# Instance norm on one core: the first store leaves as a 2 KB-per-row transfer and a 30 KB-per-row transfer

## The chip, the core and the metric

The kernel runs on one core of a Trainium2 chip. A core has four compute engines that matter here: TensorE (PE in the profile, with its weight loads as PEld), VectorE (DVE), ScalarE (ACT) and GpSimd (POOL), and SyncE (SP), which here only issues transfers. Tensors live in HBM. Work is done in the on-chip buffer SBUF, which has 128 partitions, and in the accumulation memory PSUM. Sixteen DMA engines move data between HBM and SBUF. An engine that issues transfers has a queue of them; the profile calls SP's queue q1 and ACT's queue q10, and each of the two reaches all 16 DMA engines.

The metric is the device time of one execution in microseconds (us), and lower is better.

## The reference

The input x has the shape 4 x 8 x 16 x 256 x 256 in float32: 512 channels of 65,536 numbers, 134 MB. Each channel is normalised by its own mean and variance and multiplied by its own gamma.

```python
mu = x.mean(axis=(3, 4), keepdims=True)
var = ((x - mu) ** 2).mean(axis=(3, 4), keepdims=True)
x_norm = (x - mu) / np.sqrt(var + 1e-5)
out = x_norm * gamma[None, :, :, None, None]
```

Every number is read once and written once: 134 MB in, 134 MB out.

## The kernel before

**Tiles.** The 512 channels are cut into 32 units of 16 channels. A unit is one tile `xt` of 128 partitions x 8192 float32 (4 MB): each channel takes 8 partitions, and each partition holds one row of 32 KB that is contiguous in HBM. There are six such tiles in SBUF (`slots`, `AHEAD = 6`), and unit u lives in slot u % 6.

**Start.** Line 54 issues the loads of units 0 to 5 at once: units 1 and 3 on ACT's queue, units 0, 2, 4 and 5 on SP's. Gamma comes in by a small transfer from GpSimd (line 52) and is spread over the partitions by 16 small matmuls (line 83) into `g_col`.

**The loop over units (lines 100 to 131).** For each unit:
- line 102, VectorE: the sum of each row, into `st[:, u, 0]`
- line 103, ScalarE: the sum of squares of each row, into `st[:, u, 1]`; the squares themselves go to a throw-away tile `junk`
- line 111, TensorE: a matmul with the constant `navg` adds up the 8 rows of each channel and hands every partition minus the mean and minus the mean square, in `ps`
- lines 112, 116, 120 and 122: four small operations on VectorE, ScalarE, VectorE, VectorE that give `scale` = gamma / sqrt(var + eps)
- line 125, VectorE: the tile is normalised in place
- line 129, ScalarE's queue: the store of the tile
- line 131, SP's queue (through line 48): the load of unit u + 6 into the slot that the store of unit u leaves

**What sets the order.** Each engine runs its instructions in the order in which they are written here. Waits between engines are semaphores that the framework puts in. The load of unit u + 6 waits on SP until the store of unit u has landed, as both use one slot. Every large transfer signals its landing on one of eight semaphores, which the framework hands out in turn, in the order of the program: the six first loads, the store of unit 0, the load of unit 6, the store of unit 1, the load of unit 7, and so on. Before a transfer takes a semaphore again, its issuing engine waits until the previous transfer on that semaphore has landed. For a store in the middle of the kernel that previous transfer is the store four units earlier.

In SBUF a whole tile is one row per partition, so the transfer of a tile is 128 pieces of 32 KB, eight for each DMA engine, and one 4-byte piece on each engine for the semaphore.

Of the kernel before, what the change touches and what calls it, by code (L numbers as in the profile page):

```python
# [1 line left out]

# [4 lines left out]

F32 = mybir.dt.float32
U8 = mybir.dt.uint8
ALU = mybir.AluOpType  # L10
ACTF = mybir.ActivationFunctionType
AX = mybir.AxisListType


@with_exitstack
def kernel(
    ctx: ExitStack,
    tc: tile.TileContext,
    x: bass.AP,
    gamma: bass.AP,  # L20
    out: bass.AP,
):
    nc = tc.nc
    B, G, C, H, W = x.shape
    P = nc.NUM_PARTITIONS
    HW = H * W
    n_ch = B * G * C
    S = 8
    K = P // S
    F = HW // S  # L30
    U = n_ch // K
    NG = (G * C) // K
    AHEAD = 6
    assert HW % S == 0 and (G * C) % K == 0

    xv = x.rearrange("b g c h w -> (b g c h w)").rearrange("(u p f) -> u p f", p=P, f=F)
    ov = out.rearrange("b g c h w -> (b g c h w)").rearrange("(u p f) -> u p f", p=P, f=F)
    gv = gamma.rearrange("g c -> (g c)")

    data = ctx.enter_context(tc.tile_pool(name="data", bufs=1))  # L40
    singles = ctx.enter_context(tc.tile_pool(name="singles", bufs=1))
    psum = ctx.enter_context(tc.tile_pool(name="psum", bufs=4, space=bass.MemoryType.PSUM))
    ctx.enter_context(tc.manual_schedule())

    slots = [data.tile([P, F], F32, name=f"xt{i}") for i in range(AHEAD)]

    def load(u, queue):
        queue.dma_start(out=slots[u % AHEAD][:], in_=xv[u])  # L48


    g_row = singles.tile([1, G * C], F32, name="g_row")
    nc.gpsimd.dma_start(out=g_row[:], in_=gv[None, :])  # L52
    for u in range(AHEAD):
        load(u, nc.scalar if u in (1, 3) else nc.sync)


    eps_t = singles.tile([P, 1], F32, name="eps_t")
    nc.gpsimd.memset(eps_t[:], 1e-5)  # L58
    one = singles.tile([1, 1], F32, name="one")
    nc.gpsimd.memset(one[:], 1.0)  # L60
    navg = singles.tile([P, K, S], F32, name="navg")
    nc.gpsimd.memset(navg[:], -1.0 / HW)  # L62
    nc.gpsimd.affine_select(  # L63
        out=navg[:], in_=navg[:], pattern=[[-S, K], [0, S]], compare_op=ALU.is_ge,
        fill=0.0, base=0, channel_multiplier=1,
    )
    nc.gpsimd.affine_select(  # L67
        out=navg[:], in_=navg[:], pattern=[[S, K], [0, S]], compare_op=ALU.is_ge,
        fill=0.0, base=S - 1, channel_multiplier=-1,
    )  # L70
    navg_w = navg[:].rearrange("p k s -> p (k s)")
    root_eps = singles.tile([P, 1], F32, name="root_eps")
    nc.scalar.activation(out=root_eps[:], in_=eps_t[:], func=ACTF.Sqrt)  # L73
    g_rep = singles.tile([1, NG, K, S], F32, name="g_rep")
    g_ps = psum.tile([P, NG], F32, name="g_ps", bufs=1)
    g_col = singles.tile([P, NG], F32, name="g_col")

    nc.vector.tensor_copy(  # L78
        out=g_rep[:],
        in_=g_row[:].rearrange("o (n k) -> o n k", n=NG).unsqueeze(3).to_broadcast([1, NG, K, S]),  # L80
    )
    for n in range(NG):
        nc.tensor.matmul(  # L83
            out=g_ps[:, n : n + 1],
            lhsT=g_rep[:, n].rearrange("o k s -> o (k s)"),
            rhs=one[:],
            start=True, stop=True,
        )
    nc.vector.tensor_copy(out=g_col[:], in_=g_ps[:])  # L89

    junk = singles.tile([P, F], U8, name="junk")

    st = singles.tile([P, U, 2], F32, name="st")
    nvar = singles.tile([P, U], F32, name="nvar")
    std = singles.tile([P, U], F32, name="std")
    rstd = singles.tile([P, U], F32, name="rstd")
    scale = singles.tile([P, U], F32, name="scale")

    squares = []
    for u in range(U):  # L100
        t = slots[u % AHEAD]
        nc.vector.reduce_sum(out=st[:, u, 0:1], in_=t[:], axis=AX.X)  # L102
        square = nc.scalar.activation(  # L103
            out=junk[:], in_=t[:], func=ACTF.Square, accum_out=st[:, u, 1:2],
        )
        if u:

            tc.declare_no_dep(square.ins, squares[-1].ins, reason="junk, ordered by the root between")
        squares.append(square)
        ps = psum.tile([P, 2], F32, name="ps")  # L110
        nc.tensor.matmul(out=ps[:], lhsT=navg_w, rhs=st[:, u], start=True, stop=True)  # L111
        nc.vector.tensor_scalar(  # L112
            out=nvar[:, u : u + 1], in0=ps[:, 0:1], scalar1=ps[:, 0:1],
            scalar2=ps[:, 1:2], op0=ALU.mult, op1=ALU.add,
        )
        nc.scalar.activation(  # L116
            out=std[:, u : u + 1], in_=nvar[:, u : u + 1], func=ACTF.Sqrt,
            bias=eps_t[:], scale=-1.0,
        )
        nc.vector.reciprocal(out=rstd[:, u : u + 1], in_=std[:, u : u + 1])  # L120
        g = u % NG
        nc.vector.tensor_mul(  # L122
            out=scale[:, u : u + 1], in0=rstd[:, u : u + 1], in1=g_col[:, g : g + 1],
        )
        nc.vector.tensor_scalar(  # L125
            out=t[:], in0=t[:], scalar1=ps[:, 0:1], scalar2=scale[:, u : u + 1],
            op0=ALU.add, op1=ALU.mult,
        )
        nc.scalar.dma_start(out=ov[u], in_=t[:])
        if u + AHEAD < U:  # L130
            load(u + AHEAD, nc.sync)


# [1 line left out]
_INS = ['x', 'gamma']  # L135
_OUTS = [((4, 8, 16, 256, 256), 'float32')]


# [23 lines left out]
```

## Time and profile before

| what | value |
|---|---|
| median of 7 runs | 627.2 us (626.78 to 627.54) |
| the profiled execution: its own time | 626.78 us |
| the profiled execution: span of the trace | 625.1 us |
| moved | 134.22 MB read from HBM, 134.22 MB written |
| mean rate over the span | 429 GB/s |
| VectorE busy | 443.3 us, 71% of the span |
| ScalarE busy | 238.8 us, 38% |
| TensorE busy | 21.4 us, 3% |
| first large piece starts on a DMA engine / last store's signals are written | 1.79 us / 623.75 us |

The span runs from the first to the last instruction of the trace; the 1.7 us between it and the execution's own time lie outside the trace. A busy share is an average over the whole span. The profile gives the rate of the DMA engines slice by slice; the trace also keeps a record of every piece that a DMA engine moved, with its start, its length, its bytes and its queue. Times of single pieces below are from those records, and are counted from the start of the span as the other times are.

### The profile page before, as it was taken

What the parts mean: (1) busy time and instruction counts of PE and PEld (TensorE: products, weight loads), DVE (VectorE), ACT (ScalarE), POOL (GpSimd) and SP (SyncE); (2) the same over time, 40 slices, a digit from 0 to 9 for tenths busy, and PEclk for the clock granted to TensorE, in tenths of its full rate; (3) what the DMA queues carried; (4) which work ended last, traced back from release to release, by engine and by line L of the source; (5) the groups of instructions that cost most, each with busy time, mean ns of one, the idle gap of its engine ahead of it and who ended that gap; (6) DMA issues with size and microseconds to landing.
All of it is one profiled execution on the core that took longest, in us unless ns stands there. A gap on an engine that the chain in (4) does not pass through costs nothing.

```text
span 625.1 us, 627 instructions
## 1 busy us (share of the span) xinstructions
PE 21.4 (3%) x80; PEld 19.5 (3%) x80; DVE 443.3 (71%) x162; ACT 238.8 (38%) x98; POOL 1.9 (0%) x10
## 2 busy tenths in 40 slices
PE   2000000000000000000000000000000000000000
PEld 2000000000000000000000000000000000000000
DVE  0588999999776687666786767867668676687730
ACT  0444444444443234432344423444224442244400
POOL 1000000000000000000000000000000000000000
DMA  8999999999999999999999999999999999999998
GB/s 369 436 411 428 436 436 436 436 436 435 424 432 436 433 428 434 436 434 436 436 436 421 434 434 436 430 430 436 436 434 436 436 430 426 434 436 434 426 436 369
DMA packets 9250, 268.46 MB, mean 429 GB/s; under 512 B 1056, under 2 KB 1056, under 8 KB 1056
## 3 DMA queue, kind: packets, MB, share of 16 engines
q10 hardware_dynamic: 4896, 142.61, 52.9%
q1 hardware_dynamic: 4320, 125.83, 46.8%
q14 instruction: 2, 0.02, 0.0%
q0 software_dynamic: 32, 0.00, 0.0%
HBM read 134.22 MB, written 134.22 MB: 429 GB/s over the span
## 4 chain that ended last, share of the span: by engine, by line
another core or an unknown queue 61%; DMA 17%; DVE 15%; SPq 1%; PE 1%; issue 0%; ACT 0%
DVE st L102 10%; DMA xt<-in_x_dram 10%; DMA out_dram<-xt 8%; DVE xt L125 5%; SPq L48 1%; PE ps L111 1%; ACT std L116 0%; DVE nvar L112 0%; DVE rstd L120 0%; DVE scale L122 0%
## 5 line engine op out<-in xcount | busy, mean ns | idle before, releaser
L102 DVE TENSOR_REDUCE st<-xt 128x1 f32<-128x8192 f32 x32 | 277.9, 8685 | 105.4 <-DMA xt<-in_x_dram 105.4
L103 ACT ACTIVATE junk<-xt 128x8192 uint8<-128x8192 f32 x32 | 225.0, 7030 | 275.2 <-DMA xt<-in_x_dram 232.1
L125 DVE TENSOR_SCALAR xt<-xt,ps,scale 128x8192 f32<-128x8192 f32 x32 | 145.6, 4551 | 1.2
L116 ACT ACTIVATE std<-nvar,eps_t 128x1 f32<-128x1 f32 x32 | 9.4, 295 | 79.6 <-DVE nvar L112 79.6
L111 PE MATMUL ps<-st,navg 128*128 128x2 f32 x64 | 17.9, 349 | 562.1 <-DVE st L102 562.1
L111 PEld LDWEIGHTS ps<-st,navg 128*128 128x128 f32 x64 | 16.0, 311 | 564.0 <-issue 564.0
L112 DVE TENSOR_SCALAR nvar<-ps 128x1 f32<-128x1 f32 x32 | 9.2, 287 | 23.8 <-PE ps L111 23.8
L120 DVE RECIPROCAL rstd<-std 128x1 f32<-128x1 f32 x32 | 5.3, 164 | 11.6 <-ACT std L116 11.6
L78 DVE COPY g_rep<-g_row 1x1024 f32<-1x1024 f32 x1 | 0.7, 684 | 10.4 <-DMA g_row<-in_gamma_dram 10.4
L103 ACT ACTIVATION_READ_ACCUMULATOR junk<-xt 128x1 f32 x32 | 6.0, 186 | 0.0
L122 DVE TENSOR_TENSOR scale<-rstd,g_col 128x1 f32<-128x1 f32 x32 | 5.1, 159 | 1.1
L83 PE MATMUL g_ps<-one,g_rep 1*128 1x1 f32 x16 | 3.5, 346 | 11.3 <-DVE g_rep L78 11.3
L83 PEld LDWEIGHTS g_ps<-one,g_rep 1*128 1x128 f32 x16 | 3.5, 325 | 11.2 <-issue 11.2
L89 DVE COPY g_col<-g_ps 128x8 f32<-128x8 f32 x1 | 0.2, 166 | 3.7 <-PE g_ps L83 3.7
L73 ACT ACT_TABLE_LOAD x1 | 1.3, 1283 | 1.7 <-PEq L146 1.7
L52 POOL DMA_DIRECT2D g_row<-in_gamma_dram x1 | 0.6, 609 | 0.8 <-POOLq L146 0.8
L63 POOL TENSOR_SCALAR_AFFINE_SELECT navg<-navg 128x128 f32<-128x128 f32 x1 | 0.4, 400 | 0.1
L67 POOL TENSOR_SCALAR_AFFINE_SELECT navg<-navg 128x128 f32<-128x128 f32 x1 | 0.4, 399 | 0.1
L62 POOL MEMSET navg<- 128x128 f32 x1 | 0.2, 232 | 0.0
L73 ACT ACTIVATE root_eps<-eps_t 128x1 f32<-128x1 f32 x1 | 0.2, 203 | 0.0
L58 POOL MEMSET eps_t<- 128x1 f32 x1 | 0.1, 118 | 0.0
L146 POOL MEMSET const-bfloat16-1.0<- 128x1 bf16 x1 | 0.1, 102 | 0.0
(4 smaller groups left out, 0.4 us busy)
## 6 DMA issues: line engine op xcount, KB each, us to landing
out_dram<-xt ACTq DMA_DIRECT2D x32, 4096.0 KB, 62.5
xt<-in_x_dram SPq DMA_DIRECT2D x30, 4096.0 KB, 38.5
xt<-in_x_dram ACTq DMA_DIRECT2D x2, 4096.0 KB, 31.5
g_row<-in_gamma_dram POOLq DMA_DIRECT2D x1, 0.5 KB, 9.1
```

The source lines that it names most:

```text
L48: queue.dma_start(out=slots[u % AHEAD][:], in_=xv[u])
L73: nc.scalar.activation(out=root_eps[:], in_=eps_t[:], func=ACTF.Sqrt)
L78: nc.vector.tensor_copy(out=g_rep[:], in_=g_row[:].rearrange("o (n k) -> o n k", n=NG).unsqueeze(3).to_broadcast([1, NG, K, S]),)
L83: nc.tensor.matmul(out=g_ps[:, n : n + 1], lhsT=g_rep[:, n].rearrange("o k s -> o (k s)"), rhs=one[:], start=True, stop=True,)
L102: nc.vector.reduce_sum(out=st[:, u, 0:1], in_=t[:], axis=AX.X)
L103: square = nc.scalar.activation(out=junk[:], in_=t[:], func=ACTF.Square, accum_out=st[:, u, 1:2],)
L111: nc.tensor.matmul(out=ps[:], lhsT=navg_w, rhs=st[:, u], start=True, stop=True)
L112: nc.vector.tensor_scalar(out=nvar[:, u : u + 1], in0=ps[:, 0:1], scalar1=ps[:, 0:1], scalar2=ps[:, 1:2], op0=ALU.mult, op1=ALU.add,)
L116: nc.scalar.activation(out=std[:, u : u + 1], in_=nvar[:, u : u + 1], func=ACTF.Sqrt, bias=eps_t[:], scale=-1.0,)
L120: nc.vector.reciprocal(out=rstd[:, u : u + 1], in_=std[:, u : u + 1])
L122: nc.vector.tensor_mul(out=scale[:, u : u + 1], in0=rstd[:, u : u + 1], in1=g_col[:, g : g + 1],)
L125: nc.vector.tensor_scalar(out=t[:], in0=t[:], scalar1=ps[:, 0:1], scalar2=scale[:, u : u + 1], op0=ALU.add, op1=ALU.mult,)
```

## The change

The store of unit 0 is issued as two transfers on the same queue, one after the other: the first 512 columns of every row (128 rows of 2 KB), then the other 7680 columns (128 rows of 30 KB). The stores of units 1 to 31 are as before. The bytes, the tiles and the compute instructions are the same. There is one more transfer in the program, so from there on each transfer gets the next semaphore of the eight; and the load of unit 6 has two stores to wait for.

```diff
@@ -126,7 +126,9 @@
             out=t[:], in0=t[:], scalar1=ps[:, 0:1], scalar2=scale[:, u : u + 1],
             op0=ALU.add, op1=ALU.mult,
         )
-        nc.scalar.dma_start(out=ov[u], in_=t[:])
+
+        for lo, hi in [(0, 512), (512, F)] if u == 0 else [(0, F)]:
+            nc.scalar.dma_start(out=ov[u, :, lo:hi], in_=t[:, lo:hi])
         if u + AHEAD < U:
             load(u + AHEAD, nc.sync)
 
```

## The prediction

> **What bounds the kernel now.** I read the page's slices first, then its queues, then the stretches, the waits and the chain, and last the records of single pieces.
>
> ```profile
> DVE  0588999999776687666786767867668676687730
> DMA  8999999999999999999999999999999999999998
> GB/s 369 436 411 428 436 436 436 436 436 435 424 432 436 433 428 434 436 434 436 436 436 421 434 434 436 430 430 436 436 434 436 436 430 426 434 436 434 426 436 369
> q10 hardware_dynamic: 4896, 142.61, 52.9%
> q1 hardware_dynamic: 4320, 125.83, 46.8%
> ```
>
> The DMA engines are full from the first slice to the last, while VectorE falls to about 7 tenths after slice 10. The queue rows (pieces, MB, share) say that q1 and q10 split the engines between them and leave nothing. In the records nearly all 8192 large pieces last 1.213 us, and one follows another on its engine every 1.210 us, as loads beside loads, loads beside stores, or stores alone. So 512 pieces per engine x 1.210 = 619.5 us of the 625.1 us span cannot be hidden by anything; only the other 5.6 us (first piece at 1.79, slow first pieces, the dip in slice 3, 66 signal pieces of 7 to 9 ns per engine, the end from 623.75 on) are open to any gain.
>
> The stretches show whether one queue suffices, and the only real dip (columns: length, five engines, clock, DMA share, GB/s):
>
> ```profile
> 37.00:39.00 2.00, 0.00 (x0) 0.00 (x0) 2.00 (x2) 0.97 (x1) 0.00 (x0) 1.00 1.06 459
> 39.00:41.00 2.00, 0.00 (x0) 0.00 (x0) 2.00 (x1) 2.00 (x1) 0.00 (x0) 1.00 0.84 328
> 41.00:43.00 2.00, 0.00 (x0) 0.00 (x0) 2.00 (x1) 2.00 (x1) 0.00 (x0) 1.00 0.91 262
> 43.00:45.00 2.00, 0.00 (x0) 0.00 (x0) 2.00 (x1) 2.00 (x2) 0.00 (x0) 1.00 1.21 524
> ...
> 300.00:320.00 20.00, 0.56 (x2) 0.50 (x2) 14.48 (x6) 8.06 (x4) 0.00 (x0) 1.00 1.01 434
> ...
> 595.00:615.00 20.00, 0.00 (x0) 0.00 (x0) 5.00 (x4) 0.29 (x1) 0.00 (x0) 1.00 1.02 442
> ```
>
> 300 to 320 is both queues, 595 to 615 the store queue alone: the same rate but for pieces counted where they start. From 37 to 45 the mean is (459+328+262+524)/4 = 393, so (434-393)/434 x 8 = 0.75 us is lost. That is where the first store reaches the engines: in the records the last pieces of unit 3's load take up to 1.66 us, and the first piece of unit 4's load, right ahead of the first store piece, takes 1.51 to 2.08.
>
> Waits and chain, then the instructions at the change (start, length):
>
> ```profile
> SPq L48 <- DMA out_dram<-xt: 534.6, 26, 59.5
> ...
> DVE st L102 <- DMA xt<-in_x_dram: 105.4, 24, 7.6
> ```
>
> ```profile
> 256.48 0.33 SPq L48
> 256.80 18.96 another core or an unknown queue
> 275.82 0.33 SPq L48
> ```
>
> ```profile
> 37.51 8.68 DVE L102 TENSOR_REDUCE st<-xt 128x1 f32<-128x8192 f32 x1
> 37.63 0.35 ACTq L129 DMA_DIRECT2D out_dram<-xt  x1
> 38.02 7.03 ACT L103 ACTIVATE junk<-xt 128x8192 uint8<-128x8192 f32 x1 [5.41 <-DVE xt L125]
> 44.96 0.19 ACT L103 ACTIVATION_READ_ACCUMULATOR junk<-xt 128x1 f32 x1
> ...
> 62.26 0.33 SPq L48 DMA_DIRECT2D xt<-in_x_dram  x1
> ```
>
> SP sends a load whenever a store has landed, every 19.36 us, which is 16 pieces x 1.210: eight of a load and eight of a store, in turn. VectorE's part of a unit is 14.93 us (from one L102 at 37.51 to the next at 52.44), so it waits 4.3 us per unit. The loop paces itself by the DMA engines.
>
> **The change, part by part.** The sum is made against the profiled execution (626.78 us, span 625.1), which lies 0.4 under the median; the difference is carried to the median, 627.2.
>
> Issue. ACT sends one more transfer, 0.35 us plus the 0.04 us gap to L103. Unit 1's squares then start at 38.41 instead of 38.02 and end with their read at 45.54; the row sum beside them ends at 37.51 + 8.68 = 46.19. Cover: 0.65 us left, cost nothing. Were it gone, the 0.39 us would meet VectorE, which works off loaded tiles until 157 us and waits for loads after. SP tests one semaphore more before unit 6's load (17 ns in the rows); it is off the engines' way.
>
> Pieces. Each engine moves 16 pieces and 2 signals for this store instead of 8 and 1. The bytes are the same. Nine more pieces cost between nothing and the 9 ns of a signal piece each, 0.08 us. I take 0.08.
>
> The turns. In the records the queues take turns piece by piece, whatever the bytes (a load's and a store's signals come together, 61.3 and 61.6). So eight 2 KB pieces (about 1.21/16 = 0.08 us each, an estimate by bytes) let eight 32 KB pieces of load 4 through: from 41.7, both done by 52. Then eight 30 KB pieces (1.13) go with load 5: 8 x 2.35 = 18.8, both done near 71. Store 0 lands near 71 instead of 61.65, load 5 near 71 instead of 81.2. SP's queue is then empty, for load 6 leaves SP about 0.6 us after the landing (61.65 to 62.26) and its first piece needs about 1 us (0.81 to 1.79 at the start). In those 1.6 us store 1, queued since 53, runs alone: no engine idles. Store 1 has then 1.3 pieces of lead, so each later load is sent with 1.3 x 2.42 = 3.1 us of the load before still to run, more than the 1.6 us that SP needs. Cost of the dry moment: nothing if it goes as at 585 (store queue alone), and at most the 0.75 us that the first store's arrival cost. Here nothing new begins, loads and stores have met before, so I take 0.2, near the low end.
>
> The first store's own dip stays (0.75). With small first pieces it could vanish, -0.75, or come back in some form at each turn (rival B). I take no change.
>
> Later. Loads run about 9 us earlier, so the first starved unit on VectorE is about 11 instead of 9. Stores queue deeper. A store waits on ACT for its semaphore's last user, the store four units back: four units are 77.4 us. Before, a store landed 62.5 us after its issue. Now it is due about 9 us earlier, with its load, and lands about 9 us later, as store 0 does (71 against 61.65): 80 us, so from unit 11 on each store is held about 2 us and then lands about 77 us after its issue. Behind it on ACT stand only the next squares, whose tile comes some 2 us later still; three stores are queued meanwhile, so the engines stay full. A held store is in this trace already: L125 ended at 522.97 and the store left at 527.35, squares 0.4 us late, while the pieces around it kept their 1.210 us. Cost nothing; were the cover gone, at most 2 us per unit against VectorE's wait of 4.3. At the end the last load lands near 576 (585.4) and the last store is issued near 591 (600.46), but store 30, ahead of it, ends only at 614.1, so the end is still that of the pieces.
>
> Sum: 0.08 + 0.2 = +0.28 us, 627.1 for the profiled execution, 627.5 for the median. The ends for this case: -0.75 gives 626.4; 0.08 + 0.75 and 0.3 of scatter (the 7 runs lie within 0.4 of their median) gives 628.3.
>
> A rule against the change: the Trainium skill, "DMA: Bandwidth & Descriptors", section "Anatomy of one DMA", puts a fixed cost of about 2.0 us on each DMA, mostly its write receipt. In this trace the last four stores on ACT's queue end at 594.7, 604.4, 614.1 and 623.75, 9.68 us apart, which is 8 x 1.210: behind a queued transfer the fixed cost isn't seen. By the page the sum would be 627.2 + 2.0 = 629.2; I go by the rows.
>
> **The rivals.**
> B, slower: each small piece is too short to cover the start of the next load piece. For it: the first load pieces of the kernel took up to 2.17 us and load 4's first piece at the dip about 0.6 us more than 1.21. Against: gamma's 32-byte pieces went through between load pieces at 7.2 to 7.6 us and no piece near them is longer than 1.22. Price: 8 turns x 0.6 = 4.8 us, 632.3 in full. It decides from 0.16 us per turn (1.25 in all).
> C, slower: the load queue runs dry for every unit, as its lead is 3.1 us instead of a tile, and each restart costs. At 0.6 x 25 loads, 15 us, 642. Against: the lead above, and the store queue alone at full rate.
> D, faster: the dip vanishes (-0.75) and the engines, whose last signals now spread from 622.84 to 623.75, end closer together (-0.45, half of it): 626.0.
> E, the change doesn't do what it says: if all eight small pieces go in one turn, loads gain one piece instead of eight. 627.3.
>
> **How the numbers follow.** Forecast 0.62, E 0.06, D 0.08, B 0.18, C 0.06. About 0.2% (1.25 us) can be told from no change. Same: forecast, E and a quarter of D, 0.70. Faster: the rest of D, 0.06. Slower: B and C, 0.24. The range 626.2 to 630.5 leaves out half of B, C and the lower half of D, 0.19. The likeliest alone: 626.4 to 628.3.
>
> **What would show it.** Right: the first store's two parts land near 52 and 71; load 6 leaves SP near 71.5; loads take about 21 us from issue to landing instead of 38.5 and stores about 77 instead of 62.5; L102 last starts near 576; the slices still read 9 in the DMA row; the span within 1 us. Wrong: slices 3 and 4 far below 411 and 428 (B), gaps between pieces after 72 us (C), or load 4 landing near 60 (E). The prediction falls if any engine idles with pieces queued, or if pieces of 32 KB change from 1.213 us.

## The result and the profile after

The changed kernel takes 630.61 us (median of 14 executions, 627.80 to 636.77) against 627.18 us (34 executions, 626.62 to 627.67): the ratio is 1.0076, 95% interval 1.0058 to 1.0094. By the medians it is slower by about 3.4 us, where +0.3 us was forecast, and just above the range. The scatter is part of the result: before, all executions lie within 1.1 us of each other; after, they fall into a group of eight at 628 to 631 and a group of six at 634 to 637. The median lies near the upper edge of the lower group, so it says little by itself; the ratio agrees with the means (631.9 against 627.2 us, 4.8 us apart). Slow executions, 1.5% or more above the fastest of their kernel, are left out of the ratios: one of the changed kernel at 638.57 us, which is the first one profiled, and one at 640.3 us in e0_after below.

The profile shown here is a second one of the changed kernel, taken beside the experiments (an execution of 636.90 us, span 635.2 us, of the slower group). First the page's slices and queues, as read before:

```profile
DVE  0589999999786766867668666686666867668710
DMA  9999999999999999999999999999999999999994
GB/s 378 442 415 422 415 415 433 440 433 434 429 429 429 432 423 429 437 429 433 429 437 429 427 431 429 427 429 425 442 431 431 431 429 431 433 429 427 437 429 190
q10 hardware_dynamic: 5040, 142.61, 52.1%
q1 hardware_dynamic: 4320, 125.83, 46.6%
```

The DMA engines still read 9 in every slice up to the last: on the average over the sixteen no idle time shows. But slices 5 and 6 move 415 GB/s, many later ones 425 to 431, and the last is nearly half empty (190). The instructions at the change and on SP, from the timeline:

```profile
37.59 0.83 ACTq L131 DMA_DIRECT2D out_dram<-xt  x2
38.47 7.03 ACT L103 ACTIVATE junk<-xt 128x8192 uint8<-128x8192 f32 x1 [5.89 <-DVE xt L125]
...
72.09 0.33 SPq L48 DMA_DIRECT2D xt<-in_x_dram  x1
...
89.50 0.33 SPq L48 DMA_DIRECT2D xt<-in_x_dram  x1
```

Two transfers are issued, the squares start 0.45 us later, load 6 leaves SP at 72.09. All of this is as forecast. Then the end, in stretches (the last two columns are the DMA share and GB/s), first of the kernel before, then of this profile:

```profile
600.00:622.00 22.00, 0.00 (x0) 0.00 (x0) 0.43 (x1) 0.00 (x0) 0.00 (x0) 1.00 1.00 430
622.00:626.00 4.00, 0.00 (x0) 0.00 (x0) 0.00 (x0) 0.00 (x0) 0.00 (x0) 1.00 0.21 86
626.00:634.00 8.00, 0.00 (x0) 0.00 (x0) 0.00 (x0) 0.00 (x0) 0.00 (x0) 1.00 0.00 0
```

```profile
600.00:622.00 22.00, 0.00 (x0) 0.00 (x0) 5.05 (x4) 0.29 (x1) 0.00 (x0) 1.00 1.00 430
622.00:626.00 4.00, 0.00 (x0) 0.00 (x0) 0.00 (x0) 0.00 (x0) 0.00 (x0) 1.00 0.78 336
626.00:634.00 8.00, 0.00 (x0) 0.00 (x0) 0.00 (x0) 0.00 (x0) 0.00 (x0) 1.00 0.15 66
```

Until 622 the engines are full in both. After that, in this profile, they leave one by one: at 626 to 634 only 15% of them still work, on the average. In the records of single pieces the first engine writes the last store's signal at 623.9 us, only 0.2 us after the last engine of the kernel before, and the last three at 629.9, 632.1 and 633.6. Before, the first and the last were 622.84 and 623.75. **The time that counts went into a few of the sixteen engines**: each has the same 512 pieces' worth of bytes to move, the slowest took some 10 us longer over them than the fastest, and it sets the end.

Where an engine loses time can be read from the records too, as the length of a piece above the usual one of its size. I call such a piece stretched. Averaged over the 16 engines, before lost 0.10 us between 60 and 100 us and 0.09 us from there to the end. This profile lost 1.18 and 2.52 us. There are two stages:

1. *The restart, 75 to 90 us.* Load 6 enters an SP queue that had run dry. On nine engines the store piece just ahead of its first piece takes 1.6 to 2.3 us instead of 1.21, and on nearly all a load piece of the same tile, beside the signal of store 1, takes longer too, up to 2.5. The signals of store 1 are then 3.6 us apart over the engines, where before the signals of any store lie within 0.91 us.
2. *The drift.* From 157 us on 89 load pieces, and no store piece, are stretched by 0.15 to 0.8 us. Most of them stand next to the place where one store ends and the next begins (67 of the 89 touch the signal of a store), and mostly on engines that lag already (for 54 of those 67 that signal is among the last five of its sixteen). The signals of one store grow from 3.4 us apart (105 us) to 13.1 (547 us).

### The profile page after: what moved, and what is told of

Read it like the earlier page. It is cut to its first block, busy times and chain, and to the rows that moved or that the text cites. A ratio compares the mean times of both kernels' runs of the same rounds, so it can differ in the third digit from the quotient of the medians.

```text
span 636.8 us, 629 instructions
## 1 busy us (share of the span) xinstructions
PE 21.4 (3%) x80; PEld 19.5 (3%) x80; DVE 443.1 (70%) x162; ACT 238.8 (38%) x98; POOL 1.9 (0%) x10
## 4 chain that ended last, share of the span: by engine, by line
DMA 57%; DVE 24%; another core or an unknown queue 12%; PE 1%; issue 1%; ACT 0%; SPq 0%
DMA xt<-in_x_dram 50%; DVE st L102 19%; DMA out_dram<-xt 7%; DVE xt L125 4%; PE ps L111 1%; DVE nvar L112 1%; ACT std L116 0%; DVE rstd L120 0%; DVE scale L122 0%; SPq L48 0%
## 5 line engine op out<-in xcount | busy, mean ns | idle before, releaser
L102 DVE TENSOR_REDUCE st<-xt 128x1 f32<-128x8192 f32 x32 | 277.9, 8684 | 112.2 <-DMA xt<-in_x_dram 112.2
L125 DVE TENSOR_SCALAR xt<-xt,ps,scale 128x8192 f32<-128x8192 f32 x32 | 145.6, 4551 | 1.2
```

Of the source, the lines that this page charges most:

```text
L125: nc.vector.tensor_scalar(out=t[:], in0=t[:], scalar1=ps[:, 0:1], scalar2=scale[:, u : u + 1], op0=ALU.add, op1=ALU.mult,)
```

## The experiments

All runs were timed beside the kernel before on the same chip: e1 to e4 and e12 to e15 on chip 14, e0, e5, e6 and e8 on chip 15, e7, e9, e10 and e11 on chip 3, e16 and e17 on chip 7. "Restart" is the mean stretch per engine in the 40 us or so around the restart of the load queue, "later" from there to the end, both from the records of the profiled execution; "last signals" is when the first and the last engine end. For e2_rows the first window is 60 to 100 us, for e8_tilt 175 to 240, where the odd transfers run.

| run | first store, or other edit | us, median | ratio, 95% interval | restart, later us | last signals |
|---|---|---|---|---|---|
| before | uncut | 626.78 to 627.22 | 1 | 0.10, 0.09 | 622.8, 623.8 |
| e0_after | 2 + 30 KB | 636.07 | 1.0104, 1.0065 to 1.0144 | 1.18, 2.52 | 623.9, 633.6 |
| e1_half | 16 + 16 KB | 627.19 | 1.0003, 0.9994 to 1.0013 | 0.00, 0.11 | 622.6, 623.7 |
| e7_8k24 | 8 + 24 KB | 627.19 | 1.0004, 0.9995 to 1.0013 | 0.00, 0.11 | 622.8, 623.7 |
| e9_24k8 | 24 + 8 KB | 627.27 | 1.0004, 0.9994 to 1.0013 | 0.00, 0.11 | 623.0, 624.0 |
| e6_swap | 30 + 2 KB | 627.45 | 1.0008, 0.9999 to 1.0018 | 0.12, 0.08 | 622.8, 624.5 |
| e12_4k28 | 4 + 28 KB | 632.33 | 1.0111, 1.0068 to 1.0153 | 0.96, 0.10 | 623.0, 626.2 |
| e13_1k31 | 1 + 31 KB | 628.65 | 1.0028, 1.0018 to 1.0038 | 1.40, 0.09 | 623.0, 625.4 |
| e14_last2k | last 2 KB, then first 30 KB | 635.59 | 1.0120, 1.0066 to 1.0175 | 1.59, 0.06 | 623.3, 626.0 |
| e5_dry | uncut, load queue made to run dry | 628.80 | 1.0029, 1.0018 to 1.0040 | 1.47, 0.07 | 623.7, 625.9 |
| e3_lock | 2 + 30 KB, and load 5 cut alike | 627.47 | 1.0005, 0.9996 to 1.0015 | 0.02, 0.09 | 623.2, 624.4 |
| e4_lead4 | 2 + 30 KB in 64 rows, 64 rows whole | 628.52 | 1.0031, 1.0012 to 1.0051 | 0.04, 0.11 | 623.8, 625.3 |
| e15_u1 | 2 + 30 KB at unit 1 | 629.77 | 1.0044, 1.0029 to 1.0059 | 0.56, 0.10 | 622.9, 626.9 |
| e16_u4 | 2 + 30 KB at unit 4 | 631.30 | 1.0072, 1.0043 to 1.0100 | 0.10, 1.04 | 623.2, 629.3 |
| e17_u10 | 2 + 30 KB at unit 10 | 627.53 | 1.0008, 0.9998 to 1.0017 | 0.04, 0.14 | 622.8, 624.4 |
| e10_u16 | 2 + 30 KB at unit 16 | 627.26 | 1.0006, 0.9997 to 1.0015 | 0.01, 0.02 | 622.9, 623.9 |
| e11_u16swap | 30 + 2 KB at unit 16 | 627.42 | 1.0005, 0.9995 to 1.0015 | 0.00, 0.02 | 622.8, 624.1 |
| e2_rows | 64 rows + 64 rows, uncut | 644.86 | 1.0283, 1.0235 to 1.0330 | 1.85, 10.46 | 631.5, 640.6 |
| e8_tilt | uncut, 2 pieces more on 8 engines | 635.75 | 1.0153, 1.0107 to 1.0198 | 2.25, 0.12 | 623.2, 632.3 |

The times are those of several executions, and the ratios lie nearer to the means than to the medians; the last two columns are those of one execution. In the kernels with a loss that one need not be of the same group as the median: e14_last2k's profile is of an execution of 629.22 us, while three others took 635.3 to 637.8.

**The first four: what of the change costs the time?** My theory after seeing the result was the lead: eight load pieces gained, a dry load queue, engines set apart at the restart. The rivals were the small pieces themselves, the further transfer with its shifted semaphores, and any loss of step between the ends of loads and stores.

e1_half, against the changed kernel:

```diff
-        for lo, hi in [(0, 512), (512, F)] if u == 0 else [(0, F)]:
+        for lo, hi in [(0, F // 2), (F // 2, F)] if u == 0 else [(0, F)]:
```

> The first store in two transfers of 16 KB of each row: still 16 pieces on each engine, so by the turns the same lead of eight load pieces, but no 2 KB piece. If the lead and the dry load queue after it cost the time: load 6 leaves SP near 72 us, the engines' signals for store 1 lie 2 to 4 us apart, and the time is 629 to 635 us, as with 2 KB and 30 KB. If the 2 KB pieces cost it: 627.2 to 627.6. If the one further transfer (semaphores handed out one place on, stores held on ACT) costs it: also 629 to 635, to be told apart by the next kernel.

Measured: 627.19 us, ratio 1.0003. This is the run that felled the simple theory. Its timeline shows the same lead and the same dry queue:

```profile
71.72 0.33 SPq L48 DMA_DIRECT2D xt<-in_x_dram  x1
...
87.25 0.33 SPq L48 DMA_DIRECT2D xt<-in_x_dram  x1
```

Load 6 leaves at 71.72, about as in the changed kernel (72.09), but load 7, which waits for the last engine's signal of store 1, at 87.25 instead of 89.50. The two restarts piece by piece, one engine of each kernel, from the records (start in us; L a load piece, S a store piece, * a signal, in brackets the length in ns where it is stretched):

```
16 + 16 KB: 71.08L* 71.09S* 71.09S 72.30S 73.51S 74.72S 75.93L 77.14S 78.35L 79.56S 80.77L 81.98S 83.19L 84.40S 85.61L 86.82S*
2 + 30 KB:  71.27L* 71.27S* 71.28S 72.49S 73.70S 74.91S(1302) 76.22S(2318) 78.53L(1535) 80.06S 81.27L 82.48S 83.69L 84.90S 86.11L(2061) 88.17S*
```

In both the store queue runs alone for four or five pieces, then the load comes in. These lone pieces are whole 32 KB pieces of store 1 in every kernel. What differs is what ran before them, up to 71 us, in turn with the last load pieces: the second part of store 0. "Ahead of the restart" means those pieces here and below. With 16 KB pieces ahead of it no piece is stretched; with 30 KB pieces one to four are on each engine. The windows around it say the same (71 to 80, 80 to 90 us; last column GB/s), first 16 + 16 KB, then 2 + 30 KB:

```profile
71.00:80.00 9.00, 0.56 (x2) 0.50 (x2) 7.82 (x5) 4.35 (x3) 0.00 (x0) 1.00 1.03 444
80.00:90.00 10.00, 0.00 (x0) 0.00 (x0) 10.00 (x2) 7.12 (x2) 0.00 (x0) 1.00 0.97 419
```

```profile
71.00:80.00 9.00, 0.56 (x2) 0.50 (x2) 7.82 (x5) 4.26 (x3) 0.00 (x0) 1.00 1.05 430
80.00:90.00 10.00, 0.00 (x0) 0.00 (x0) 10.00 (x2) 7.12 (x2) 0.00 (x0) 1.00 1.00 403
```

VectorE's work is equal to the hundredth; only the rate differs. So the lead, the dry queue, the further transfer and the offset of ends are all present in e1_half, and together they cost nothing measurable.

e2_rows:

```diff
-        for lo, hi in [(0, 512), (512, F)] if u == 0 else [(0, F)]:
-            nc.scalar.dma_start(out=ov[u, :, lo:hi], in_=t[:, lo:hi])
+        for a, b in [(0, 64), (64, P)] if u == 0 else [(0, P)]:
+            nc.scalar.dma_start(out=ov[u, a:b], in_=t[a:b])
```

> The first store in two transfers of 64 whole rows: eight pieces on each engine as before, one signal piece more, one transfer more in the program, stores held as in the changed kernel only if they come later. If the lead costs the time: no lead, load 6 leaves SP near 62.5, 627.2 to 627.5. If the further transfer and the shifted semaphores cost it: 629 to 635. If already one turn of offset between the ends of loads and stores is enough to set the engines apart: above 628.5.

Measured: 644.86 us, the slowest of all, though no piece is small, there is no lead of eight, and load 6 left SP at 66.7. The stretch where the second half goes out and the next whole tile follows:

```profile
60.00:66.00 6.00, 0.56 (x2) 0.50 (x2) 4.82 (x5) 0.53 (x3) 0.00 (x0) 1.00 0.94 279
```

279 GB/s: in the records store and load pieces of 2.1 to 3.0 us lie side by side there on most engines, the signals come out 3.2 us apart, and drift follows to the end. None of the three forecasts had this cause. One turn of offset can't be it, since e1_half has more. It may be that a transfer of 64 rows hands an engine other rows than a transfer of 128 does; the records hold no addresses, and it was not tried by itself.

e3_lock, on top of the change:

```diff
     for u in range(AHEAD):
+        if u == 5:
+            for lo, hi in [(0, 512), (512, F)]:
+                nc.sync.dma_start(out=slots[u][:, lo:hi], in_=xv[u, :, lo:hi])
+            continue
         load(u, nc.scalar if u in (1, 3) else nc.sync)
```

> The first store in 2 KB and 30 KB of each row as in the changed kernel, and the load of unit 5 cut in the same way, so that its 16 pieces take back the lead: store 0 and the 2 KB part of load 5 end together, store 1 and the 30 KB part end together. If the lead costs the time: 627.2 to 627.8, signals of store 1 within 1 us. If small pieces cost it: there are twice as many, 631 to 637.

Measured: 627.47 us, 1.0005. Load 6 left SP at 63.34. Twice as many 2 KB and 30 KB pieces, and no loss once the load queue doesn't run dry: the small pieces by themselves are cleared, and with the lead and the dry queue gone the change costs nothing measurable.

e4_lead4:

```diff
-        for lo, hi in [(0, 512), (512, F)] if u == 0 else [(0, F)]:
-            nc.scalar.dma_start(out=ov[u, :, lo:hi], in_=t[:, lo:hi])
+        if u == 0:
+            nc.scalar.dma_start(out=ov[u, 0:64, 0:512], in_=t[0:64, 0:512])
+            nc.scalar.dma_start(out=ov[u, 0:64, 512:F], in_=t[0:64, 512:F])
+            nc.scalar.dma_start(out=ov[u, 64:P], in_=t[64:P])
+        else:
+            nc.scalar.dma_start(out=ov[u], in_=t[:])
```

> Only rows 0 to 63 of the first store are cut into 2 KB and 30 KB: 12 pieces and three signals on each engine, a lead of four to six load pieces, so the load queue still holds 5 to 10 us of work when load 6 is sent. If the dry load queue and its restart cost the time: 627.2 to 627.8 and the signals of store 1 within 1 us. If it is enough that loads and stores no longer end together: 629 to 635.

Measured: 628.52 us, 1.0031, between the two forecasts. Its loss lies before 60 us (2.1 us of stretch between 30 and 60, against 0.8 before), where its 64-row transfers run, and nothing is lost afterwards. That is an execution of 628.58 us; one of the ten took 634.48, and of that one there is no profile. After e2_rows it says little on the lead; as a test it was spoilt by its own rows.

**The second four: the dry restart, the order, and a lag by itself.**

> The changed kernel once more, beside the next three on one chip. 628 to 637 us as before; load 6 leaves SP near 72, the engines' signals for store 1 lie 3 to 4 us apart, and the last signals 5 us or more.

Measured: 636.07 us; of ten executions four took 628.7 to 629.7 and six 635.6 to 640.3. Its views are those above. The last signals were 9.7 us apart.

e5_dry, against the kernel before:

```diff
-        if u + AHEAD < U:
-            load(u + AHEAD, nc.sync)
+        for v in {0: [], 1: [1, 0]}.get(u, [u]):
+            if v + AHEAD < U:
+                load(v + AHEAD, nc.sync)
```

> The kernel before, with the first store in one piece, and the load of unit 7 sent ahead of the load of unit 6, so that SP waits for store 1 and its queue runs dry near 81 us while store 2 and 3 are queued. If a dry load queue and its restart are enough to set the engines apart: 629 to 640 us, signals of the next store more than 2 us apart. If the restart does harm only when the engines already differ, or only beside pieces that are cut unequally: 627.2 to 627.8, signals within 1.2 us.

Measured: 628.80 us, a shade under the 629 written for this case, 1.0029 with an interval of 1.0018 to 1.0040, and the signals of the next store 3.2 us apart. Nothing is cut here: **a dry load queue restarted behind whole 32 KB store pieces is enough for the first stage.** 39 pieces are stretched by over 150 ns around it and two later, as in the kernel before, which has two after 100 us; the seven executions lie within 0.8 us. So it has the restart's loss without the drift.

e6_swap cuts `(0, F - 512), (F - 512, F)`.

> The first store as 30 KB of each row and then 2 KB of each row: the same pieces, the same lead and the same dry load queue near 71 us, but 2 KB pieces and not 30 KB pieces ahead of the restart. If the 30 KB pieces ahead of the restart (stretched on a few engines near 63 us) set the engines apart: 627.2 to 627.8. If any unequal cut with a dry queue does: 629 to 636.

Measured: 627.45 us, 1.0008. The same pieces, the same lead and the same dry moment (load 6 at 72.6 us) with the 2 KB pieces last, and nothing measurable lost. So the order of the two parts matters, which is what stands ahead of the restart.

e8_tilt, against the kernel before:

```diff
         nc.scalar.dma_start(out=ov[u], in_=t[:])
+        if u in (6, 7):
+            nc.scalar.dma_start(out=ov[u + 16, 0:8], in_=t[0:8])
```

> The kernel before, with two further stores of 8 rows of 32 KB after the stores of units 6 and 7, into places that units 22 and 23 overwrite later: two pieces more, 2.42 us, on 8 of the 16 engines, nothing else, no lead, no dry queue. If a lag once there stays as it is: 627.2 + 2.4 = 629.6 us, last signals about 3 us apart. If engines that lag by more than a piece fall back further: above 632 us.

Measured: 635.75 us, which is what the second theory wrote, but not for its reason. Around the two further transfers store pieces took 1.5 to 4.9 us, not 1.21. On the slowest engine they took 4.9 and 4.5, together 9.4 us, which is about the whole difference (the first engine ends at 623.2, the last at 632.3). From 236 to 546 us the signals of one store are 14 us apart (9.1 us at the end, where the store queue runs alone), and 0.12 us of stretch per engine came from 240 us to the end. The stretches show it, full until 600 and a third busy at the end:

```profile
240.00:600.00 360.00, 11.16 (x40) 10.02 (x40) 267.48 (x100) 143.80 (x60) 0.00 (x0) 1.00 1.00 433
623.00:633.00 10.00, 0.00 (x0) 0.00 (x0) 0.00 (x0) 0.00 (x0) 0.00 (x0) 1.00 0.32 138
```

This lag alone didn't grow; that theory fell too.

**The third four: how large must the pieces be?** The edits change only the pair of column ranges, or the unit in which the cut is made (`u == 16`).

> The first store as 8 KB and then 24 KB of each row: same number of pieces, same dry load queue near 71 us, 24 KB pieces ahead of the restart. If the size of the pieces ahead of the restart decides (2 KB and 16 KB gave no loss, 30 KB gives 2 to 10 us): between, 627.5 to 630, signals of store 1 between 0.4 and 3.5 us apart. If a 2 KB piece must come first: 627.2 to 627.6.

> The first store as 24 KB and then 8 KB of each row: 8 KB pieces ahead of the restart. If the size of the pieces ahead of the restart decides: 627.2 to 627.8, no stretched piece between 70 and 90 us. If any cut at a quarter or less does harm: 628.5 or more.

Measured: 627.19 and 627.27 us, no stretched piece at either restart. The forecast had put 8 + 24 KB at 627.5 to 630 if the size decides; 24 KB pieces ahead of the restart cost nothing measurable. If the size decides, the loss sets in above them, not in proportion.

> The cut in 2 KB and 30 KB is made in the store of unit 16 instead of the first. If the lead with 30 KB pieces ahead of a dry load queue sets the engines apart wherever it falls: stretched pieces some 5 us after that store has landed (near 410 us), the time 628.5 to 634, less than with the first store since half the kernel is left for the engines to fall behind. If it needs the first store (the first time that loads and stores meet): 627.2 to 627.6.

> The same at unit 16 with the 30 KB transfer first and the 2 KB transfer last. If the order decides as it did at the first store: 627.2 to 627.8. If away from the start both orders act alike: the same as the kernel beside it.

Measured: 627.26 and 627.42 us. At unit 16 the queue ran just as dry (in the records no load piece starts from 380 to 386 us, load 22 is sent at 382.45), with the 30 KB pieces ahead, and nothing was stretched. My forecast for e10_u16 was a loss; it was wrong. One reserve holds for all four of these runs: they were made on chip 3, and no kernel with a loss was timed there. That a chip without the loss would show the same was not excluded.

**The last six**, to settle whether size, address or place decides.

> The first store as 4 KB and then 28 KB of each row. If the size of the pieces decides, with 8 + 24 free of loss and 2 + 30 at 629 to 640: between, 627.2 to 632. If it needs exactly a very small first piece: 627.2 to 627.6.

> The first store as 1 KB and then 31 KB of each row. If the size of the pieces decides, at least the loss of 2 + 30: 629 to 640. If 2 + 30 is a chance meeting of turns: 627.2 to 628.

> The first store as the last 2 KB of each row and then the first 30 KB: the same sizes, order and turns as the changed kernel, other addresses. If sizes and order decide: 629 to 640. If the start of the 30 KB pieces at 2 KB into the row decides: 627.2 to 627.8.

Measured: 632.33, 628.65 and 635.59 us, all slower. The address does not decide: the 30 KB pieces of e14_last2k start at the beginning of the rows. With 2, 8, 16 and 24 KB pieces ahead of the first restart there is no loss to speak of (0.00 to 0.12 us of stretch per engine), with 28, 30, 31 and 32 KB (e5_dry) there is, 1.0 to 1.6 us of stretch per engine each time. A forecast missed: 1 + 31 did not lose more than 2 + 30. Its nine executions lie between 628.1 and 630.0; it has the restart's loss, and none of them shows the drift.

> The cut in 2 KB and 30 KB made in the store of unit 1. If it needs the first store, where loads and stores first meet: 627.2 to 627.8. If any cut of this kind while VectorE still works off its first tiles does it: 629 to 640.

> The cut in 2 KB and 30 KB made in the store of unit 4, while VectorE still works off loaded tiles without a wait. If VectorE's unbroken reading and writing of tiles is what stretches pieces at the restart: 628.5 or more, engines 2 us or more apart afterwards. If only the first one or two stores are touched: 627.2 to 627.8.

> The cut in 2 KB and 30 KB made in the store of unit 10, where VectorE waits for loads, as at unit 16. 627.2 to 627.8 if it is the stretch without waits that matters or the first stores; 628.5 or more if unit 16 was the exception.

Measured: 629.77, 631.30 and 627.53 us. The loss does not need the first store; it is there at units 0, 1 and 4 and not at 10 and 16. That falls together with the stretch in which VectorE still works off its first tiles, but the windows speak against VectorE as the cause:

```profile
380.00:400.00 20.00, 0.56 (x2) 0.50 (x2) 18.82 (x7) 10.18 (x4) 0.00 (x0) 1.00 1.02 439
```

That is the cut at unit 16 around its restart: VectorE is nearly as busy (18.82 of 20 us) as around the restart at the start of the kernel (10.00 of 10), because the lead has brought its loads forward, and the rate is full. And unit 4 lost its time otherwise than unit 0: hardly at the restart (0.10 us), but in a drift later (1.04 us).

**What is shown and what stays open.** Shown: the time is the slowest engine's. Shown too: when the cut is kept and the load queue doesn't run dry, the loss is gone (e3_lock); a load queue that runs dry without any cut has the restart's loss (e5_dry); one that runs dry behind small pieces has none (e1 on the chip of e12 to e14, e6 on that of e0 and e5). The limit between 24 and 28 KB, and that the cut is free at unit 16, rest on chip 3 alone; e17_u10, on chip 7 beside e16_u4, agrees that late in the kernel the cut costs nothing measurable. In the profiled executions the rest is the drift: those at 629 us (e12_4k28, e14_last2k) have the restart's loss and none later, and those at 636.9 and 638.6 us have both.

Open: why a piece is stretched at a restart behind 28 KB pieces and not behind smaller ones; why not at units 10 and 16; and what starts the drift, which came, to judge by the times, in about half of the executions of the 2 + 30 KB cut and has no counterpart in engines merely set apart (e8_tilt). A rival to the size stands, too. In e1, e7 and e9 the first load piece comes in behind the fourth lone store piece on every engine, by 76.5 us; in e0, e13 and e14 it comes behind the fifth on most. So the moment of the restart within the turns differs along with the size. In e6 about half of the engines have the fifth and none is stretched there, so the count alone is not it, but no run changed one and kept the other. No version beat the kernel before: the best of the cuts lie within 0.1% of it.

## Why the prediction was wrong

**What bounds the kernel: right, but not whole.** The bound is the pieces of 32 KB, back to back, on all engines. It was read as one pool of engines, though. The sum had no term for one engine falling behind the others, and that term is the result. The sign that the prediction named for its own fall also came: pieces of 32 KB changed from 1.213 us, 29 of them around the restart and 89 later by more than 0.15 us.

**Issue: right.** 0.45 us on ACT (squares at 38.47 instead of 38.02; forecast 38.41), hidden.

**Pieces: right.** A 2 KB piece took 84 ns and a 30 KB piece 1138, together 9 ns more than the 1213 of a 32 KB piece. Eight of these and a signal are 0.08 us, the number in the sum.

**The turns: right in the order, wrong in one size.** Pieces take turns one to one whatever their bytes, the last signals of the store's two parts came at 52.6 and 71.5 us (forecast: 52 and 71), load 6 left at 72.09 (71.5). But its first piece was not moving 1 us after the issue; on an engine without stretch it came at 77.2, 5 us later, behind five store pieces. The 1 us had been taken from the start of the kernel, where no pieces were queued. So store 1 gained four to five pieces and not 1.3, and each later load is sent while about that many pieces of the load before are still to run: loads take 29 us from issue to landing (forecast 21), stores 72.5 (77). The last L102 was to start near 576 us instead of 585.40. It started at 590.45 here, where the last load had to wait for the slowest engine, and at 579.3 in e1_half, where no engine lagged.

**The first store's dip: right in size, not in place.** Between 30 and 60 us the mean stretch is 0.79 us per engine, against 0.77 before. But it lies at 50 to 52 us, on the load pieces beside the signals of the 2 KB transfer and of load 4, and no longer at 40 to 42.

**The dry moment: the step that failed.** It was bounded by nothing and by 0.75 us, the first store's dip, and taken at 0.2, "near the low end", as nothing new begins there. The runs showed this in its place: the mean stretch around the restart is 1.18 us per engine in this profile and 1.39 in the first one, and it is uneven: some engines lost 0.2 us and some over 2. An uneven loss costs its largest share, not its mean: over the whole kernel the mean stretch from 60 us on is 3.7 us here, and the last engine ends 9.9 us later than before. The restart alone makes about 2 us (e5_dry and e13_1k31, whose profiles have no drift: 628.80 and 628.65 us). The drift that followed in about half of the executions makes the rest; the prediction had no term for it, and what starts it stays open. The nearest row was rightly chosen and wrongly read: the dip in the trace of before at 40 to 42 us had pieces stretched by 0.1 to 0.9 us too, but left the engines together, for the signals of the first store come within 0.32 us of each other.

**Held stores: they did not come.** As the stores land 72.5 us after their issue and not 77 or more, they stay under the 77.4 us of four units. Unit 11, the first that was to be held, shows it: its store leaves 0.03 us after the end of L125.

```profile
206.00 4.55 DVE L125 TENSOR_SCALAR xt<-xt,ps,scale 128x8192 f32<-128x8192 f32 x1
...
210.58 0.34 ACTq L131 DMA_DIRECT2D out_dram<-xt  x1
```

So it is for all stores but that of unit 27, which left 4.7 us after its L125, and 4.4 us after it in the kernel before. That step cost nothing, as forecast, though for another reason.

**The rivals.** B, that each small piece exposes the load piece behind it, is refuted: at 42 to 50 us the 2 KB pieces go through at 84 ns between load pieces of 1.21 (one of 1.27), and e3_lock has twice as many without a loss. It gave 632.3 in full, near the result, with the wrong mechanism; that nearness is luck, and so is that half of the fourteen executions lie inside the range, whose upper part stood for B. C named the right place, the restart, but as a loss in each of 25 units, 15 us; it happened once, and what followed was a drift on few engines. D and E did not occur.

**The page's rule.** The Trainium skill's 2.0 us for each DMA ("DMA: Bandwidth & Descriptors", section "Anatomy of one DMA", whose heading and fit are for transfers that GpSimd issues, while ScalarE issues this one) would have given 629.2. e1_half, e7_8k24 and e9_24k8 have that further transfer and differ from before by a ratio of 1.0003 or 1.0004, some 0.2 us, so the fixed cost doesn't show for a transfer with others queued around it. Another place of that page bears more on this case: its section "Why a DMA increments its semaphore by 16 and not by 1" says that the engines of a transfer finish independently, and that only the full count means that all data has landed. The trace agrees. The signals of store 1 ran from 85.5 to 89.1 us, and load 7 left SP at 89.50, after the last of them.

## What to carry to other kernels

When a kernel is bound by its DMA engines, ask not only whether they are all busy, but whether they all end together: look at the last slice, and at how far apart the signals of one transfer are. Cutting a transfer by columns gives the other queue as many turns as there are new pieces, which can run it dry; the cut itself is nearly free (0.08 us here), the restart of the dry queue beside a running one may not be (0 to about 2 us here, uneven over the engines, and in some executions a drift after it). Transfers of fewer rows than the others were costlier in this kernel: 18 us for two halves of one tile, 9 us for two further transfers of eight rows.

## What was not expected of the hardware

- A load queue that is restarted beside a running store queue gets its first piece moving about 4 to 5 us after the issue (71.72 to 75.9 with 16 KB pieces before, 72.09 to 77.2 with 30 KB), against 1.0 us at the start of the kernel.
- Engines that had lost step didn't find it again, although SP waits for the slowest of them in every unit: in e8_tilt the signals of one store were 14 us apart at 236 us and still at 546 us. The engines ahead had stores queued to go on with, for the DMA share is 1.00 from 240 to 600 us.
- Around two further transfers of eight rows of 32 KB from neighbouring partitions, one row on each of eight engines, store pieces took 1.5 to 4.9 us instead of 1.21 (e8_tilt).
